# Average pooling over 512 MB: 56 KB blocks in three buffers with a store each, in place of 64 KB loads in two buffers with a store for every four

## The chip, the cores and the metric

The kernel runs on one core of a Trainium2 chip. Three of its engines do work here: VectorE (DVE in the profile), ScalarE (ACT) and SyncE (SP), which only issues transfers. Sixteen DMA engines carry the data between HBM, where input and output lie, and SBUF, the core's own memory of 128 partitions. The metric is the device time of one execution in microseconds (us); lower is better. MB and GB are powers of ten; KB is 1,024 bytes, as in the profile.

## The reference

The input is float32, 64 x 256 x 8192. Each output element is the mean of four neighbours along the last axis, without overlap:

```python
for i in range(out_len):            # out_len = 2048
    start = i * stride              # stride 4, kernel_size 4
    output[:, :, i] = np.mean(x[:, :, start : start + kernel_size], axis=2)
```

So 536.87 MB are read and 134.22 MB are written, and nothing is used twice. Since four neighbours in memory make one output, the input may be cut anywhere at a multiple of four, and the whole problem is one flat array of 134,217,728 elements, 1,048,576 for each partition.

## The kernel before

The flat array is cut into 16 groups. In a group each partition owns 8 rows, that is 256 KB that are contiguous in HBM, and the group is fetched in four loads (`LOADS = 4`, `W = 16384` elements): a load brings 64 KB to each partition, from 128 places that lie 256 KB apart. It makes 8.39 MB. There are 64 such loads; the last of them is split into five pieces (`pieces`: 8192, 4096, 2048, 1024 and 1024 elements for each partition).

For a load, `sums` adds even and odd neighbours on VectorE (line 65, written back over the first half of the input tile), adds even and odd neighbours of that again into the output tile (line 72), and multiplies by 1/4 on ScalarE in place (line 83). The last two pieces are scaled on VectorE instead (line 79). The output tile `ot` holds a whole group, 64 KB for each partition. Only after the group's fourth load, whose second addition is cut into four (`LAST_CUTS`), does one store of 8.39 MB write it out (`store`, line 86). For the last group the store is split into five: one of 4,096 KB while the last loads run, and four more behind them.

All transfers, loads (line 59) and stores (line 86), are issued by SyncE and so go through one DMA queue, in the order in which SyncE gets to them. There are two input tiles (`bufs=2`) and one output tile (`bufs=1`). A load waits until VectorE has read the tile it overwrites: load k+2 is issued when line 72 is done with block k. The first line 72 of a group waits until the store of the group before has landed, because it overwrites the one output tile. Tiles, semaphores and waits come from the framework; the order of issue is the one written in the loop.

Of the kernel before, what the change touches and what calls it, by code (L numbers as in the profile page):

```python
# [1 line left out]

# [4 lines left out]


LOADS = 4

LAST_CUTS = 4


@with_exitstack
def kernel(
    ctx: ExitStack,
    tc: tile.TileContext,
    x: bass.AP,
    kernel_size: bass.AP,
    stride: bass.AP,  # L20
    out: bass.AP,
):
    nc = tc.nc
    K, S = int(kernel_size), int(stride)
    assert K == S == 4
    B, C, L = x.shape
    P = nc.NUM_PARTITIONS
    add = mybir.AluOpType.add
    dt = x.dtype

    per = B * C * L // P
    W = 16384
    G = W * LOADS
    V = W // K
    groups = per // G
    assert per == groups * G

    xf = x.flatten_outer_dims()
    of = out.flatten_outer_dims()
    rows = G // L  # L40
    R = P * rows

    def xg(g):
        return xf[g * R : (g + 1) * R].rearrange("(p f) m -> p (f m)", f=rows)

    def og(g):
        return of[g * R : (g + 1) * R].rearrange("(p f) m -> p (f m)", f=rows)

    pin = ctx.enter_context(tc.tile_pool(name="xin", bufs=2))
    pout = ctx.enter_context(tc.tile_pool(name="res", bufs=1))  # L50

    state = {}

    def load(g, l, a, b):

        if a == 0:
            state["xt"] = pin.tile([P, W], dt, name="xt")
        xt = state["xt"]
        nc.sync.dma_start(out=xt[:, a:b], in_=xg(g)[:, l * W + a : l * W + b])  # L59
        return xt  # L60

    def sums(xt, ot, l, a, b, cuts, scale_on_dve=False):

        h = (a, (a + b) // 2)
        nc.vector.tensor_tensor(  # L65
            out=xt[:, h[0] : h[1]], in0=xt[:, a:b:2], in1=xt[:, a + 1 : b : 2], op=add
        )
        n = (b - a) // K
        for c in range(cuts):
            lo, hi = c * n // cuts, (c + 1) * n // cuts  # L70
            o = ot[:, l * V + a // K + lo : l * V + a // K + hi]
            nc.vector.tensor_tensor(  # L72
                out=o,
                in0=xt[:, a + 2 * lo : a + 2 * hi : 2],
                in1=xt[:, a + 2 * lo + 1 : a + 2 * hi : 2],
                op=add,
            )
            if scale_on_dve:
                nc.vector.tensor_scalar(  # L79
                    out=o, in0=o, scalar1=1.0 / K, scalar2=None, op0=mybir.AluOpType.mult  # L80
                )
            else:
                nc.scalar.mul(o, o, 1.0 / K)  # L83

    def store(g, ot, a, b):
        nc.sync.dma_start(out=og(g)[:, a:b], in_=ot[:, a:b])  # L86

    todo = [(g, l) for g in range(groups) for l in range(LOADS)]  # L90
    last = todo[-1]
    pieces = [W // 2, W // 4, W // 8, W // 16, W // 16]
    tiles = {}
    ot = None
    tiles[0] = load(*todo[0], 0, W)
    tiles[1] = load(*todo[1], 0, W)
    for k, (g, l) in enumerate(todo[:-1]):
        if l == 0:
            held, ot = ot, pout.tile([P, G // K], dt, name="ot")
        sums(tiles.pop(k), ot, l, 0, W, LAST_CUTS if l == LOADS - 1 else 1)  # L100
        if l == LOADS - 1:
            store(g, ot, 0, G // K)
        if k + 2 < len(todo) - 1:
            tiles[k + 2] = load(*todo[k + 2], 0, W)
        elif k + 2 == len(todo) - 1:

            n = pieces[0]
            lt = load(*last, 0, n)
            store(g, ot, 0, (l + 1) * V)
            for w in pieces[1:]:  # L110
                load(*last, n, n + w)
                n += w
    g, l = last
    store(g, ot, (l - 1) * V, l * V)
    edges = [sum(pieces[:i]) for i in range(len(pieces) + 1)]
    for a, b in zip(edges[:3], edges[1:4]):
        sums(lt, ot, l, a, b, 1)
    store(g, ot, l * V, l * V + edges[3] // K)
    for a, b in zip(edges[3:-1], edges[4:]):
        sums(lt, ot, l, a, b, 1, scale_on_dve=True)  # L120
    store(g, ot, l * V + edges[3] // K, (l + 1) * V)


# [1 line left out]
_INS = ['x', 'kernel_size', 'stride']  # L125
_OUTS = [((64, 256, 2048), 'float32')]

_NUMBERS = {'kernel_size': 4, 'stride': 4}


# [26 lines left out]
```

## Time and profile before

| what | value |
|---|---|
| median of 3 runs | 1558.77 us (1558.01 to 1560.35) |
| profiled execution, its time | 1560.02 us |
| profiled execution, its span | 1558.2 us (so 1.8 us lie around it) |
| instructions | VectorE 183, ScalarE 112 |
| DMA packets | 12,532, of which 1,392 under 512 bytes |
| loads / stores issued | 68 / 19, all by SyncE |

The span runs from the first instruction to the last event that the profiler saw. A DMA is split over 16 engines; each engine gets the rows of 8 partitions, one packet for each row, and one packet of 4 bytes that reports completion. So a DMA makes 128 + 16 = 144 packets, and 87 of them make 12,528, which is the packet count of the queue that SyncE uses. In the timeline a row gives the start, the duration, the engine, the line and the tile; in brackets stands the idle time before it and what ended that.

### The profile page before, as it was taken

What the parts mean: (1) busy time and instruction counts of PE and PEld (TensorE: products, weight loads), DVE (VectorE), ACT (ScalarE), POOL (GpSimd) and SP (SyncE); (2) the same over time, 40 slices, a digit from 0 to 9 for tenths busy, and PEclk for the clock granted to TensorE, in tenths of its full rate; (3) what the DMA queues carried; (4) which work ended last, traced back from release to release, by engine and by line L of the source; (5) the groups of instructions that cost most, each with busy time, mean ns of one, the idle gap of its engine ahead of it and who ended that gap; (6) DMA issues with size and microseconds to landing.
All of it is one profiled execution on the core that took longest, in us unless ns stands there. A gap on an engine that the chain in (4) does not pass through costs nothing.

```text
span 1558.2 us, 522 instructions
## 1 busy us (share of the span) xinstructions
DVE 844.0 (54%) x183; ACT 241.9 (16%) x112; POOL 0.2 (0%) x4
## 2 busy tenths in 40 slices
DVE  3654636546365463654636546365463654636546
ACT  1111201112011120111201112011120111201111
POOL 0000000000000000000000000000000000000000
DMA  9999999999999999999999999999999999999998
GB/s 424 437 404 431 442 434 436 434 431 434 429 432 432 439 436 434 432 434 431 431 431 436 436 439 431 434 432 434 431 431 431 431 431 431 431 432 436 426 440 369
DMA packets 12532, 671.13 MB, mean 431 GB/s; under 512 B 1392, under 2 KB 1392, under 8 KB 1776
## 3 DMA queue, kind: packets, MB, share of 16 engines
q1 hardware_dynamic: 12528, 671.09, 99.8%
q14 instruction: 4, 0.03, 0.0%
HBM read 536.87 MB, written 134.22 MB: 431 GB/s over the span
## 4 chain that ended last, share of the span: by engine, by line
DMA 71%; DVE 27%; ACT 1%; SPq 0%; issue 0%
DMA xt<-in_x_dram 71%; DVE xt L65 18%; DVE ot L72 9%; ACT ot L83 1%; SPq L86 0%; SPq L59 0%; DVE ot L79 0%
## 5 line engine op out<-in xcount | busy, mean ns | idle before, releaser
L65 DVE TENSOR_TENSOR xt<-xt 128x8192 f32<-128x8192 f32 (+2 forms) x68 | 556.9, 8190 | 542.5 <-DMA xt<-in_x_dram 542.5
L83 ACT ACTIVATE ot<-ot 128x1024 f32<-128x1024 f32 (+3 forms) x111 | 240.6, 2167 | 1306.1 <-DVE ot L72 1302.6
L72 DVE TENSOR_TENSOR ot<-xt 128x1024 f32<-128x1024 f32 (+4 forms) x113 | 286.9, 2572 | 164.1 <-DMA out_dram<-ot 162.4
L83 ACT ACT_TABLE_LOAD x1 | 1.3, 1283 | 0.7 <-PEq L138 0.7
L79 DVE TENSOR_SCALAR ot<-ot 128x256 f32<-128x256 f32 x2 | 0.6, 291 | 0.0
L138 POOL MEMSET const-bfloat16-1.0<- 128x1 bf16 x1 | 0.1, 101 | 0.0
L138 POOL MEMSET const-uint8-127<- 128x1 uint8 x1 | 0.1, 101 | 0.0
L138 POOL MEMSET const-float32-0.0<- 128x1 f32 x1 | 0.1, 98 | 0.2 <-issue 0.2
L138 POOL MEMSET const-float32-1.0<- 128x1 f32 x1 | 0.1, 98 | 0.0
## 6 DMA issues: line engine op xcount, KB each, us to landing
xt<-in_x_dram SPq DMA_DIRECT2D x1, 4096.0 KB, 17.0
out_dram<-ot SPq DMA_DIRECT2D x1, 4096.0 KB, 23.0
xt<-in_x_dram SPq DMA_DIRECT2D x1, 2048.0 KB, 27.4
out_dram<-ot SPq DMA_DIRECT2D x1, 2048.0 KB, 18.4
out_dram<-ot SPq DMA_DIRECT2D x1, 1792.0 KB, 8.0
xt<-in_x_dram SPq DMA_DIRECT2D x1, 1024.0 KB, 29.4
xt<-in_x_dram SPq DMA_DIRECT2D x2, 512.0 KB, 30.6
xt<-in_x_dram SPq DMA_DIRECT2D x63, 26.9
```

The source lines that it names most:

```text
L65: nc.vector.tensor_tensor(out=xt[:, h[0] : h[1]], in0=xt[:, a:b:2], in1=xt[:, a + 1 : b : 2], op=add)
L72: nc.vector.tensor_tensor(out=o, in0=xt[:, a + 2 * lo : a + 2 * hi : 2], in1=xt[:, a + 2 * lo + 1 : a + 2 * hi : 2], op=add,)
L79: nc.vector.tensor_scalar(out=o, in0=o, scalar1=1.0 / K, scalar2=None, op0=mybir.AluOpType.mult)
L83: nc.scalar.mul(o, o, 1.0 / K)
L138: nc = _bacc.Bacc("TRN2", target_bir_lowering=False, num_devices=1)
```

## The change

The array is now cut into 78 blocks. Each block is contiguous in HBM from its first to its last element: the 128 partitions' rows lie side by side (`"(p m) -> p m"` over a flat slice). A first block of 2,048 elements for each partition is followed by 72 blocks of 14,336 (56 KB for each partition, 7.34 MB) and by a tail of 6144, 4096, 2048, 1280 and 768, which share one input tile and one output tile. There are three input tiles of 56 KB and two output tiles of 14 KB. Every block is stored by itself as soon as ScalarE has scaled it. The stores are issued by ScalarE, behind the multiplication, through ScalarE's own DMA queue; only those of the last full block and of the first tail block are issued by SyncE, behind all loads. Line numbers of the new kernel: load 62, first addition 71, second addition 72, scaling 80 (76 for the last block, on VectorE), store 85.

```diff
-LOADS = 4
-LAST_CUTS = 4
+FULL = 14336
+BUFS_IN = 3
+BUFS_OUT = 2
+HEAD = (2048,)
+TAIL = (6144, 4096, 2048, 1280, 768)
...
-    pin = ctx.enter_context(tc.tile_pool(name="xin", bufs=2))
-    pout = ctx.enter_context(tc.tile_pool(name="res", bufs=1))
+    blocks = [(w, i == 0) for i, w in enumerate(HEAD)]
+    blocks += [(FULL, True)] * (rest // FULL)
+    blocks += [(w, i == 0) for i, w in enumerate(TAIL)]
+    n = len(blocks)
+    first = n - len(TAIL)
+    pin = ctx.enter_context(tc.tile_pool(name="xin", bufs=BUFS_IN))
+    pout = ctx.enter_context(tc.tile_pool(name="res", bufs=BUFS_OUT))
...
+    def load(i):
+        w, fresh = blocks[i]
+        if fresh:
+            load.tile, load.at = pin.tile([P, FULL], dt, name="xt"), 0
+        a = load.at
+        load.at += w
+        src = xf[P * begins[i] : P * begins[i + 1]].rearrange("(p m) -> p m", p=P)
+        xs[i] = load.tile[:, a : a + w]
+        nc.sync.dma_start(out=xs[i], in_=src)
...
+    def store(engine, i, o):
+        dst = of[P * begins[i] // K : P * begins[i + 1] // K]
+        engine.dma_start(out=dst.rearrange("(p m) -> p m", p=P), in_=o)
+
+    loaded = 0
+    for i in range(n):
+        while loaded < n and (loaded < i + BUFS_IN or loaded > first):
+            load(loaded)
+            loaded += 1
+        o = means(i)
+        store(nc.sync if i in (first - 1, first) else nc.scalar, i, o)
```

The arithmetic of a block (`means`) is that of `sums` without cuts: two additions on VectorE and one multiplication, on ScalarE for all blocks but the last.

More of the change, by code (lines that the diff above doesn't have):

```diff
@@ L26 @@
     B, C, L = x.shape
+    assert L % K == 0
     P = nc.NUM_PARTITIONS
+    dt = x.dtype
     add = mybir.AluOpType.add
[L29 to L47, printed above, removed]
@@ L49 @@
-    pin = ctx.enter_context(tc.tile_pool(name="xin", bufs=2))
-    pout = ctx.enter_context(tc.tile_pool(name="res", bufs=1))
[L52 to L64, printed above, removed]
+    xf = x.rearrange("b c l -> (b c l)")
@@ new lines @@
+    of = out.rearrange("b c l -> (b c l)")
+    rest = B * C * L // P - sum(HEAD) - sum(TAIL)
+    assert rest % FULL == 0
+    blocks = [(w, i == 0) for i, w in enumerate(HEAD)]
[5 more added lines that the diff above has]
+    pout = ctx.enter_context(tc.tile_pool(name="res", bufs=BUFS_OUT))
+    xs, begins = {}, [0]
+    for w, _ in blocks:
+        begins.append(begins[-1] + w)
@@ new lines, in load, with means @@
+    def load(i):
[7 more added lines that the diff above has]
+        nc.sync.dma_start(out=xs[i], in_=src)
+    def means(i):
+        w, fresh = blocks[i]
+        if fresh:
+            means.tile, means.at = pout.tile([P, FULL // K], dt, name="ot"), 0
+        a = means.at
+        means.at += w // K
+        o, xt = means.tile[:, a : a + w // K], xs.pop(i)
+        nc.vector.tensor_tensor(out=xt[:, : w // 2], in0=xt[:, ::2], in1=xt[:, 1::2], op=add)
@@ L65, in sums @@
         nc.vector.tensor_tensor(
-            out=xt[:, h[0] : h[1]], in0=xt[:, a:b:2], in1=xt[:, a + 1 : b : 2], op=add
+            out=o, in0=xt[:, : w // 2 : 2], in1=xt[:, 1 : w // 2 : 2], op=add
         )
[L68 to L76, printed above, removed]
-            )
[L78 to L121, printed above, removed]
+        if i == n - 1:
+            nc.vector.tensor_scalar(
+                out=o, in0=o, scalar1=1.0 / K, scalar2=None, op0=mybir.AluOpType.mult
+            )
+        else:
+            nc.scalar.mul(o, o, 1.0 / K)
@@ L125 @@
+        return o
+    def store(engine, i, o):
[8 more added lines that the diff above has]
+        store(nc.sync if i in (first - 1, first) else nc.scalar, i, o)
 _INS = ['x', 'kernel_size', 'stride']
```

## The prediction

> **What bounds the kernel now.** I read the page's busy times and slices first, then its DMA part and its chain of the work that ended last, then that chain in order of time, the groups by shape, and the timeline of the last 30 us.
>
> ```profile
> DVE 844.0 (54%) x183; ACT 241.9 (16%) x112; POOL 0.2 (0%) x4
> ...
> DMA  9999999999999999999999999999999999999998
> GB/s 424 437 404 431 442 434 436 434 431 434 429 432 432 439 436 434 432 434 431 431 431 436 436 439 431 434 432 434 431 431 431 431 431 431 431 432 436 426 440 369
> ...
> q1 hardware_dynamic: 12528, 671.09, 99.8%
> ...
> HBM read 536.87 MB, written 134.22 MB: 431 GB/s over the span
> ```
>
> No compute engine is busy for much more than half of the span, while the 16 DMA engines are busy for 99.8% of it, in every slice. The rate is the same in slices that hold a store and in those that hold only loads. So the DMA engines are the bound, and an edit counts only if it alters the bytes (it doesn't: 671.09 MB before and after), the cost of a packet, or the time in which an engine has no packet.
>
> The chain of work, in order of time, gives the pace:
>
> ```profile
> 567.21 8.70 DVE xt L65
> ...
> 625.20 8.70 DVE xt L65
> ...
> 663.90 8.70 DVE xt L65
> ...
> 760.79 8.70 DVE xt L65
> ...
> 857.49 8.70 DVE xt L65
> ```
>
> Line 65 starts when its load has landed. From 625.20 to 663.90 there are two loads and no store: 19.35 us for 8.39 MB, or 433.5 GB/s. From 567.21 to 663.90, from there to 760.79 and from there to 857.49 each stretch holds four loads and one store, five transfers of 8.39 MB: 96.69, 96.89 and 96.70 us, where five load periods would be 96.75. Over the 13 such stretches from 178.92 to 1439.86 the mean is 97.00, the least is 96.69 (four of them are 96.69 or 96.70) and the greatest is 97.73; the first one, from 80.69, took 98.23. So a store runs at the pace of a load, and turning from loads to a store and back costs nothing by itself in four stretches; the others carry an irregular loss, 0.3 us in the mean. All 14 together lie 5.5 us above 14 times 96.69.
>
> The trace also has a record of each DMA packet. Their median durations are 159 ns for 4,096 bytes, 611 for 16,384, 1,213 for 32,768 and 2,418 for 65,536. From the first to the last 61,440 bytes cost 2,259 ns: 27.2 GB/s for each engine, 435 GB/s for 16. What is left of a packet beyond its bytes is 8.4 ns; the starts of successive packets of one engine lie about 4 ns closer than the durations, so that 4 to 8 ns remain. A completion packet takes 9 ns. At 435.2 GB/s the bytes alone take 1542.0 us: of a span of 1558.2 only 16 us are anything else.
>
> **The change, part by part.**
>
> *Contiguous blocks.* A packet is still one partition's row, now 57,344 bytes in place of 65,536 for a load, 14,336 in place of 65,536 for a store. What may change is the rate at which HBM serves them. The 64 KB packets, taken from places 256 KB apart, run at the same 27.2 GB/s as the 4 KB packets: there is no loss from the layout to win back. I count nothing. The page "DMA: Bandwidth & Descriptors" of the Trainium skill (Latency and other measured facts) says that copies lose rate when the rows of the partitions lie a large power of two apart, 207 in place of 214 GB/s at 512 KiB, and advises to lay tiles out contiguously. By it some of the pitch of 256 KB might be worth up to 3%, an estimate from that page; the 2,418 ns of the packets here show none of it.
>
> *More DMAs.* 68 loads and 19 stores become 78 and 78, so 87 DMAs become 156. Each engine gets 69 x 8 = 552 more data packets and 69 more completion packets: 552 x 4.4 to 8.4 ns = 2.4 to 4.6 us, and 69 x 9 ns = 0.6 us. Together 3.0 to 5.3 us; I take **+4**, for the load period of 19.35 us lies 75 ns above its bytes' 19.275, where eight packets and a completion at 8.4 and 9 ns make 76 and at 4.4 and 9 ns make 44. The same page of the skill (Anatomy of one DMA) has a rule that speaks against the change: a DMA costs about 2.0 us beside its bytes, and DMAs are to be few and large. By it, 69 more DMAs would cost 138 us, an estimate from that page. The rows contradict it for queued DMAs, with 0.08 us each; the 2 us are paid only by a DMA that somebody waits for while nothing else is queued.
>
> *Third input buffer.* VectorE on a block, between the rows of the groups by shape:
>
> ```profile
> L65 DVE TENSOR_TENSOR xt<-xt 128x8192 f32<-128x8192 f32 x63 | 547.6, 8693 | 537.0 <-DMA xt<-in_x_dram 537.0
> L72 DVE TENSOR_TENSOR ot<-xt 128x4096 f32<-128x4096 f32 x48 | 212.4, 4425 | 163.5 <-DMA out_dram<-ot 162.4
> L83 ACT ACTIVATE ot<-ot 128x4096 f32<-128x4096 f32 x48 | 173.6, 3616 | 1103.5 <-DVE ot L72 1103.5
> ```
>
> With 4,418 ns for 4,096 elements at line 65, and 2,292 and 1,909 for 2,048 at lines 72 and 83, the sizes 7,168 and 3,584 come to 7.62 + 3.89 = 11.5 us on VectorE and 3.2 on ScalarE. A block's transfers take (7.34 + 1.84 MB) / 433.5 = 21.2 us. Load i+2 goes out when VectorE is done with block i-1, 11.5 us after that landed; load i then has 9.7 us to run and load i+1 is queued whole. So the queue never empties by some 30 us. Before, the margin was 19.35 - 13.1 = 6.2 us (line 65 waits about 6.2 us for each load); it too was enough, so the third buffer removes no idle time: 0 us. Were this cover gone, each microsecond of lateness beyond 30 would cost one per block, 72 in all.
>
> *Stores on ScalarE's queue.* The waits of SyncE's store for ScalarE (339.1 us in 18 times) leave SyncE's order. They held back loads, as at 95.17, where the store goes out before the next load; but DMA stayed busy through it, so 0 us come back. On ScalarE a store's issue waits for its own multiplication, and behind it stands only the next multiplication, some 20 us later. Line 72 waited 162.4 us for the landing of the one output tile; this goes, and it was hidden. Two output tiles are enough: a store goes out about 15 us after its block landed, and its tile is wanted 2 x 21.2 + 7.6 = 50 us after. Even if its packets alternate one for one with load packets, it runs for the whole 21 us of a period; 14 us remain.
>
> What the trace does not show is two queues that feed an engine at once. From below: a second queue could hide what lies between packets, at most the 16 us by which the span exceeds its bytes, less about 3 for start and end: -13. From above: the irregular losses could come with each store, 5.5 / 14 = 0.39 us, and 63 more stores would cost 25. A price for every packet that alternates is excluded by the four stretches without loss. I take 0, the nearest row: both directions were in flight in the last 25 us before too, at the same packet durations.
>
> *The tail.* Before:
>
> ```profile
> 1549.63 0.29 DVE L79 TENSOR_SCALAR ot<-ot 128x256 f32<-128x256 f32 x1
> 1549.83 0.42 DVE L72 TENSOR_TENSOR ot<-xt 128x256 f32<-128x256 f32 x1
> 1550.29 0.29 DVE L79 TENSOR_SCALAR ot<-ot 128x256 f32<-128x256 f32 x1
> ```
>
> VectorE ends 7.7 us before the span does; in that time the engines write the last two stores, and by the packet records the last engine ends some 2 us after most. After: let A be the landing of the last full block. The tail's loads land by A + 21, with the store before them in between. VectorE does the last full block until A + 11.5 and the tail's pieces until about A + 25. The stores that SyncE and ScalarE issue from A + 15 on keep the engines busy until A + 29.6 (8.4 us for 3.67 MB behind the loads). VectorE is done 5 us before that, so the tail stays full. I count 0, and the same unevenness of the engines as before.
>
> **Sum.** Span 1558.2 + 4 = 1562.2 us, the profiled execution's time 1560.0 + 4 = 1564.0. The median of the runs lies 1.25 below that execution, so I predict **1562.8 us**, 0.26% slower. About 0.2%, 3.1 us, is what a measurement of this kernel can tell from no change: 1555.7 to 1561.9 count as the same.
>
> **Rivals.**
>
> 1. *The irregular losses shrink* (not slower). They stand at the stores; many small contiguous stores, spread evenly, may avoid them. For it: 98.23 and 97.73 beside 96.69 at the same work. Against: nothing says what they are. If all 5.5 us go, the time is 1558.8 + 4 - 5.5 = 1557.3, the same. It decides as soon as more than 0.9 us of them go.
> 2. *Faster.* Beyond these losses, the last engines' 2 us go as well and the packets cost only 3.0: 1558.8 + 3.0 - 7.5 = 1554.3. With the gaps between packets hidden by the second queue it could reach 1546.
> 3. *Every store brings its loss*: 0.39 us x 63 = 25, so 1587; half of that is 1575. For it: the losses stand where a store starts or ends. Against: four stretches without any.
> 4. *The queue runs dry*, because stores take more than twice a period and VectorE waits for output tiles. Against: 14 us of margin there and 30 at the loads. 1 us for each of 72 blocks would be 1635.
> 5. *The change does nothing* but rearrange a saturated resource, packet costs overlapping too: 1558.8, the same.
>
> **Chances.** The forecast, 1560 to 1566: 0.43, of which 0.31 slower and 0.12 the same. Rivals 1 and 5 together, 1555.7 to 1560: 0.25, the same. Rival 2: 0.13, faster. Rival 3: 0.15, and rival 4: 0.04, slower. So faster 0.13, the same 0.37, slower 0.50. The range leaves out most of rival 2, the upper half of rival 3 and rival 4: 1555 to 1575.
>
> **What would show it.** In the profile after: 22,464 packets in the two queues (156 x 144), DMA at 9 in every slice, 431 GB/s or a little under; line 71 waiting for its load and for nothing else, one block each 21.2 us; no wait of line 72 for a store; packets of 57,344 bytes at about 2.12 us and of 14,336 at 0.535. Wrong are: packets longer than that (rival 3), gaps in DMA (rival 4), a block period under 21.1 us (rival 2).

## The result, and the profile after

| | median | range | runs |
|---|---|---|---|
| before | 1559.51 us | 1558.01 to 1560.35 | 20 |
| after | 1556.57 us | 1556.35 to 1556.79 | 20 |

After takes 0.9982 of the time of before (95% interval 0.9977 to 0.9988): 2.9 us or 0.18% less, where 0.26% more was forecast. The time lies inside the predicted range and inside what the prediction called the same. It also scatters less, by 0.4 us in place of 2.3. The page of the profile after answers to the first lines shown of before:

```profile
DVE 843.6 (54%) x157; ACT 235.1 (15%) x78; POOL 0.2 (0%) x4
...
DMA  9999999999999999999999999999999999999999
GB/s 411 437 426 429 443 432 425 442 440 418 441 440 419 440 441 421 436 443 425 431 443 427 429 442 435 422 442 441 417 440 441 422 435 443 423 433 439 432 428 395
...
q1 hardware_dynamic: 11520, 539.50, 80.2%
q10 hardware_dynamic: 10944, 131.60, 19.8%
...
HBM read 536.87 MB, written 134.22 MB: 432 GB/s over the span
```

The DMA engines are the bound as before. There are now two queues, SyncE's (q1) and ScalarE's (q10), with 22,464 packets between them. The last slice, 369 GB/s before, has 395. The view of waits lists what stopped VectorE:

```profile
DVE xt L71 <- DMA xt<-in_x_dram: 697.3, 73, 15.4
...
DVE ot L72 <- DVE xt L71: 0.4, 1, 0.4
```

The second addition waits for no store any more; the first one waits for its load, and that is all. In VectorE's timeline the loads land in an even beat:

```profile
612.58 7.62 DVE L71 TENSOR_TENSOR xt<-xt 128x7168 f32<-128x7168 f32 x1 [9.57 <-DMA xt<-in_x_dram]
...
633.74 7.62 DVE L71 TENSOR_TENSOR xt<-xt 128x7168 f32<-128x7168 f32 x1 [9.55 <-DMA xt<-in_x_dram]
...
654.91 7.62 DVE L71 TENSOR_TENSOR xt<-xt 128x7168 f32<-128x7168 f32 x1 [9.56 <-DMA xt<-in_x_dram]
```

A period is 21.17 us for 9.18 MB, whose bytes alone take 21.08 at 435.2 GB/s: 0.09 us for a block's two DMAs, sixteen data packets and two completions on each engine. Load packets still take 2.116 us and store packets 0.535, and by their records an engine takes one of each in turn.

Since the engines hardly ever rest, the right account is the time that bytes do not explain: at each moment, the time since the start of the span less the bytes moved so far at 435.2 GB/s. From the packet records of one profiled execution each (us); a packet counts as too long when it takes 0.1 us or more beyond its bytes at 27.2 GB/s and 8.4 ns:

```
                    at 240  at 480  at 1200  at 1545  last packet | packets 0.1 us or more too long
before                4.8     5.7     9.0      12.3      15.0     |   169
after                 4.1     5.2     8.2       9.9      11.4     |    33
e1_stores_on_sync     5.4     6.9    10.0      11.7      15.0     |   124
e3_two_inputs         4.3     5.3     8.3      10.0      11.5     |    47
e4_half_loads         4.8     6.5    11.6      14.1      16.9     |    50
e8_pairs              4.3     5.0    14.9      22.5      26.5     |   509
e9_64k_blocks         4.5     5.4     8.1       9.6      11.1     |    72
e10_pairs_56k         5.5     8.0    13.7      16.2      18.2     |   460
e12_half_blocks       5.0     7.0    13.1      15.9      18.4     |    51
e13_body_on_sync      5.3     6.6     9.9      11.6      13.9     |   138
e14_tail_on_sync      4.2     5.3     8.3      10.0      12.5     |    43
```

After is ahead of before by 0.7 us at 240, by 0.8 at 1200, by 2.5 at 1545 and by 3.6 at the end. In the long middle, 240 to 1200, both lose the same 4.1 us. The difference is made before 240, after 1200, and in the last 10 us.

The same records split it into three parts. What the packets too long take beyond their due, summed and divided by 16 engines, is 5.2 us in before and 0.7 in after: 4.5 less. What is left of the account at 1545 is 7.1 and 9.1: 2.0 more, for 69 more DMAs. In the last 10 us an engine stands idle for 2.4 us in the mean in before and for 1.1 in after: 1.3 less.

### The profile page after: what moved, and what is told of

Read it like the earlier page. It is cut to its first block, busy times and chain, and to the rows that moved or that the text cites. A ratio compares the mean times of both kernels' runs of the same rounds, so it can differ in the third digit from the quotient of the medians.

```text
span 1554.7 us, 658 instructions
## 1 busy us (share of the span) xinstructions
DVE 843.6 (54%) x157; ACT 235.1 (15%) x78; POOL 0.2 (0%) x4
## 4 chain that ended last, share of the span: by engine, by line
DVE 53%; another core or an unknown queue 42%; DMA 5%; issue 0%; DVEq 0%; SPq 0%
DVE xt L71 35%; DVE ot L72 18%; DMA xt<-in_x_dram 5%; DVEq L72 0%; SPq L62 0%; DVE ot L76 0%
## 5 line engine op out<-in xcount | busy, mean ns | idle before, releaser
L71 DVE TENSOR_TENSOR xt<-xt 128x7168 f32<-128x7168 f32 (+3 forms) x78 | 558.4, 7160 | 697.3 <-DMA xt<-in_x_dram 697.3
L80 ACT ACTIVATE ot<-ot 128x3584 f32<-128x3584 f32 (+3 forms) x77 | 233.8, 3037 | 1311.7 <-DVE ot L72 1311.7
L72 DVE TENSOR_TENSOR ot<-xt 128x3584 f32<-128x3584 f32 (+3 forms) x78 | 285.4, 3660 | 7.0 <-DVE xt L71 0.4
```

Source lines behind the costliest of these rows:

```text
L71: nc.vector.tensor_tensor(out=xt[:, : w // 2], in0=xt[:, ::2], in1=xt[:, 1::2], op=add)
L72: nc.vector.tensor_tensor(out=o, in0=xt[:, : w // 2 : 2], in1=xt[:, 1 : w // 2 : 2], op=add)
```

## The experiments

Three theories at first. **Q**: ScalarE's own queue removes the irregular losses, since the engines no longer turn from loads to stores as a body. **L**: the contiguous layout does. **B**: the third input buffer does. Each experiment ran beside the kernel before on one chip; ratios are to that. After itself ran only for the result, so "more than after" compares medians from different sessions; the medians of before in them lie between 1558.2 and 1559.7.

**e1_stores_on_sync.** All stores back in the loads' queue:

```diff
-        store(nc.sync if i in (first - 1, first) else nc.scalar, i, o)
+        store(nc.sync, i, o)
```

> The kernel after, with every store issued by SyncE, so that loads and stores share one queue again. Theory Q (two queues: packets of loads and stores alternate, so the engines never turn from one direction to the other as a body, and the irregular losses of before vanish): the losses come back, 1560 to 1564 us and slow packets at each store. Theory L (the contiguous layout removed them) and theory B (the third input buffer, a load always queued well ahead): as after, 1556 to 1557.5.

1560.24 us, ratio 1.0008 (0.9999 to 1.0017): 3.7 us slower than after, as Q said. But the run was not as clean as its expectation supposed. Its timeline ends so:

```profile
1542.74 1.50 DVE L71 TENSOR_TENSOR xt<-xt 128x640 f32<-128x640 f32 x2 [0.32 <-DMA xt<-in_x_dram]
1548.10 4.17 DVE L72 TENSOR_TENSOR ot<-xt 128x1536 f32<-128x1536 f32 x5 [3.85 <-DMA out_dram<-ot]
1549.89 3.31 ACT L80 ACTIVATE ot<-ot 128x1536 f32<-128x1536 f32 x4 [12.76 <-DVE ot L72]
1551.40 4.22 SPq L85 DMA_DIRECT2D out_dram<-ot  x5
1552.30 0.26 DVE L76 TENSOR_SCALAR ot<-ot 128x192 f32<-128x192 f32 x1
```

The tail's loads are issued together, and in the one queue a store stands behind them; the tail's output tile is free only when that store has landed, at 1548. VectorE is done at 1552.6, in place of 1548.0 in after. So e1 holds two effects; e13 and e14 part them below.

**e2_strided_rows.** The full blocks taken from groups in which each partition owns 224 KB:

```diff
+        group = flat[at : at + P * Q // k].rearrange("(p m) -> p m", p=P)
+        return group[:, l * FULL // k : (l + 1) * FULL // k]
```

> The kernel after, with the full blocks taken four at a time from a group in which each partition owns 224 KB, so that a load's rows lie 224 KB apart and a store's 56 KB apart; sizes, queues and buffers as after. Theory L: the losses come back in full, 1560 to 1564 us. Theories Q and B: as after, 1556 to 1557.5.

1556.46 us, ratio 0.9981 (0.9972 to 0.9990), as after. L falls: rows 224 KB apart cost nothing here. The 256 KB of before were not run in the new kernel; for them there are only before's packets, 2,418 ns for 64 KB.

**e3_two_inputs.** `BUFS_IN = 2`.

> The kernel after with two input buffers in place of three. A load then goes out 11.5 us after its forerunner landed, with 9.7 us of the next load still to run. Theory B: losses come back, above 1559 us. Theories Q and L: as after, 1556 to 1557.5, since the queue of loads never empties.

1556.55 us, ratio 0.9983 (0.9974 to 0.9991), as after. B falls.

**e4_half_loads.** Each full load cut into two DMAs:

```diff
-        nc.sync.dma_start(out=xs[i], in_=src)
+            nc.sync.dma_start(out=xs[i][:, : w // 2], in_=src[:, : w // 2])
+            nc.sync.dma_start(out=xs[i][:, w // 2 :], in_=src[:, w // 2 :])
```

> The kernel after with each full load cut into two DMAs of 28 KB for each partition: 72 more DMAs, 576 more data packets for each engine. This measures the price of a DMA, which the prediction took as 44 to 76 ns. By 44 ns 3.2 us more than after, about 1559.8; by 76 ns 5.5 us more, about 1562; if a second queue hides the gaps between packets, under 1 us more.

1562.10 us, 5.5 more than after: 77 ns for each added load, of which the account shows some 60 in the body and the rest at the end.

Then Q was tried in the frame of the kernel before, against a rival **S**: the small, frequent store is what helps, in whatever queue.

**e5_each_sync and e6_each_scalar.** Before, with a store after each load, from SyncE or from ScalarE:

```diff
-        if l == LOADS - 1:
-            store(g, ot, 0, G // K)
+        if g < groups - 1:
+            store(g, ot, l * V, (l + 1) * V)                # e5
+            nc.scalar.dma_start(out=og(g)[:, l * V : (l + 1) * V], in_=ot[:, l * V : (l + 1) * V])  # e6, in its place
```

> The kernel before, with a store of 16 KB for each partition after each load (in all groups but the last), issued by SyncE as before: 45 more DMAs, 3.5 us at 77 ns each. Theory Q (two queues): the losses stay, 1559.6 + 3.5 = 1563 us. Rival S (the small, frequent store removes the losses, the queue does not matter): 1559.6 + 3.5 - 6 = 1557.

> The same as e5_each_sync, but these stores are issued by ScalarE on its own queue. Theory Q: the losses go, 1559.6 + 3.5 - 6 to 8 = 1555 to 1557 us, at least 4 us less than e5_each_sync. Rival S: the same time as e5_each_sync.

e5 took 1562.12 us, ratio 1.0042 (1.0018 to 1.0066), with runs from 1558.7 to 1576.0: no gain in time from small stores by themselves, and S falls. e6 took 1698.38, ratio 1.0896 (1.0882 to 1.0911). Neither theory had that. The DMA part of e5's page has for these stores (count, KB each, median us to landing):

```profile
out_dram<-ot SPq DMA_DIRECT2D x61, 2048.0 KB, 12.2
```

The same part of e6's page:

```profile
out_dram<-ot ACTq DMA_DIRECT2D x60, 2048.0 KB, 35.1
```

And the view of waits of e6:

```profile
DVE ot L72 <- DMA out_dram<-ot: 251.8, 15, 16.9
```

Here a store that shares the engines with loads, one packet each, lands nearly three times as late. The kernel before has one output tile for four blocks: line 72 then waits for the last store of the group, the next load goes out late because line 72 frees its tile, and with two input tiles the engines run empty (396 GB/s over the span). This is the prediction's rival 4, in another kernel.

**e7_big_scalar.** Before, the 15 big stores from ScalarE's queue:

```diff
-            store(g, ot, 0, G // K)
+            nc.scalar.dma_start(out=og(g), in_=ot)
```

> The kernel before with nothing changed but the queue of the 15 stores of 8.39 MB: ScalarE issues them. No DMA is added. Theory Q alone: the losses go at no price, 1552 to 1554 us. Against it stands the one output tile: the store now shares the engines with loads one packet each and takes about 39 us in place of 19, so line 72 waits for it and the next load may go out too late; if that shows, 1555 us or more, with a long wait of line 72 and gaps in the DMA slices.

1672.15 us, ratio 1.0717 (1.0702 to 1.0733). The wait of line 72 that was feared came, 403.5 us in 15 times or 26.9 each, where before has 10.8. It says nothing of Q.

**e8_pairs.** A version meant to be better: 64 KB blocks, two blocks to a store.

```diff
-FULL = 14336
-BUFS_IN = 3
+FULL = 16384
+BUFS_IN = 2
...
+            if full(i) % 2:
+                nc.scalar.dma_start(out=dst, in_=means.tile)      # 32 KB for each partition
```

> A new version: blocks of 64 KB for each partition in two input buffers, the stores of two blocks joined (32 KB for each partition) in two output buffers, ScalarE's queue, head and tail as after: 107 DMAs in place of 156. By 77 ns for each of the 49 DMAs less than after it takes 3.8 us less, 1552.8; by 44 ns 2.2 less, 1554.4. If small stores are what removes the losses, 1556 or more.

1569.64 us, ratio 1.0071 (1.0059 to 1.0083), with no wait for any store. So **Q as I had put it fell**: a second queue with ample buffers, and the account shows 22.5 us unexplained at 1545, 509 packets too long. They stand where a store sets in, that is, where its first packets go out: from 647 to 655, say, where the engines take up the store issued at 643.8. A store of 32 KB packets runs for 29 of the 49 us of a pair and then stops. In after a store takes 8 x 2.645 = 21.2 us, as long as its block: the stream of stores never stops. That was theory **C**, the losses come where a stream of stores sets in or stops, with rival **P**: packets of 64 KB beside a second queue are to blame.

Not every set-in costs, though. Of e8's 31, the first one made 16 load packets too long, 1.0 us of each engine's time. The next ten, from 115 to 550 us, have two such packets between them, and at 480 the account of e8 stands at 5.0, not above after's 5.2. The loss starts at about 600 and is then some 0.7 us for each store.

**e9_64k_blocks.** After with `FULL = 16384`, `BUFS_IN = 2`, a store for each block.

> The kernel after with blocks of 64 KB for each partition in two input buffers, and still one store for each block (16 KB for each partition) from ScalarE's queue: 138 DMAs in place of 156. Theory C (the losses stand where a stream of stores sets in or stops; a store for each block, in a queue of its own, lasts as long as the block's load, so that it never stops): no losses, 18 DMAs less at 77 ns, 1555.2 us. Rival P (the losses of e8_pairs came from packets of 64 KB beside a second queue): 1560 us or more.

1555.89 us, ratio 0.9983 (0.9974 to 0.9992). No losses with 64 KB packets: P falls. The 18 DMAs saved don't show in the ratio, so it is no better version that can be told from after.

**e10_pairs_56k.** e3 with the stores of two blocks joined as in e8.

> e3_two_inputs (56 KB blocks, two input buffers) with the stores of two blocks joined, 28 KB for each partition; 36 DMAs less. The store now runs for some 25 us of the 42 us of a pair. Theory C: the losses come with each of the 36 stores, 0.3 to 0.5 us each as in e8_pairs, so 1556.6 - 2.8 + 11 to 18 = 1565 to 1572. Rival P: none, 1553.8.

1563.82 us, ratio 1.0032 (1.0021 to 1.0044): 7.3 more than e3, with 36 DMAs less. Theory C had the direction, its size was a little high. The beat shows the store's set-in and stop, 42.5 us for the pair shown:

```profile
612.17 7.62 DVE L82 TENSOR_TENSOR xt<-xt 128x7168 f32<-128x7168 f32 x1 [5.37 <-DMA xt<-in_x_dram]
...
637.72 7.62 DVE L82 TENSOR_TENSOR xt<-xt 128x7168 f32<-128x7168 f32 x1 [13.94 <-DMA xt<-in_x_dram]
...
654.67 7.63 DVE L82 TENSOR_TENSOR xt<-xt 128x7168 f32<-128x7168 f32 x1 [5.40 <-DMA xt<-in_x_dram]
```

One load shares the engines with the store and takes 25.5 us, the next has them to itself and takes 16.95.

Of the time lost in packets too long, 84% in e8 and 82% in e10 lie within 6 us of a store's first packet, about an eighth of the time. So it is the set-in of a joined store that costs, not its whole run, and at the stop the records show no loss. But theory C is too wide, and e4 shows it. There a load's packets are half as large, so that a store's eight packets are through after 8 x (1.062 + 0.535) = 12.8 us of a block's 21.2. The DMA part of e4's page has for these stores:

```profile
out_dram<-ot ACTq DMA_DIRECT2D x71, 1792.0 KB, 16.8
```

The page of after:

```profile
out_dram<-ot ACTq DMA_DIRECT2D x71, 1792.0 KB, 27.6
```

The stream of e4 stops and sets in again with each of these stores, and after 100 us e4 has six packets too long in all. A stop by itself costs nothing there. The joined stores also have packets twice as large, longer pauses, and loads whose rows lie 128 KB (e8) or 112 KB (e10) apart; which of these makes a set-in cost, no run separates.

**e11_loads_alone.** No stores of the body:

```diff
-        store(nc.sync if i in (first - 1, first) else nc.scalar, i, o)
+        if not 1 <= i < first - 1:
+            store(nc.sync if i in (first - 1, first) else nc.scalar, i, o)
```

> The kernel after without the stores of the head and the full blocks except the first block and the last full one: 71 outputs of 1.84 MB are computed and not written, 85 DMAs and 540.8 MB remain, in one queue almost throughout. By 435.2 GB/s the bytes take 1242.6 us; with 85 DMAs at 77 ns, start, end and what lies around the span (5.5 us) 1254.6 us. If one queue loses time even without any turn from loads to stores, 1258 us or more; theory C: 1254 to 1255.

1256.82 us, all runs within 0.02: 2 us over the estimate and over theory C's 1254 to 1255, but under the rival's bound. Its timeline:

```profile
616.90 7.62 DVE L71 TENSOR_TENSOR xt<-xt 128x7168 f32<-128x7168 f32 x1 [5.32 <-DMA xt<-in_x_dram]
...
633.86 7.63 DVE L71 TENSOR_TENSOR xt<-xt 128x7168 f32<-128x7168 f32 x1 [5.34 <-DMA xt<-in_x_dram]
...
650.79 7.62 DVE L71 TENSOR_TENSOR xt<-xt 128x7168 f32<-128x7168 f32 x1 [5.31 <-DMA xt<-in_x_dram]
```

Loads alone in one queue keep a period of 16.945 us, 79 ns over their bytes' 16.866, and after the first 53 us only four packets are too long.

**e12_half_blocks.** `FULL = 7168`, four input and four output buffers: twice the loads and twice the stores.

> The kernel after with blocks of 28 KB for each partition in four input and four output buffers (the tail's five pieces in two tiles): 72 more loads, 72 more stores of 7 KB packets, and the stream of stores still runs as long as the loads. This prices a store DMA where e4_half_loads priced a load. If a load costs 77 ns beyond its bytes and a store beside it almost nothing (10 ns, from the block periods of after and of e11_loads_alone), 6.3 us more than after, 1562.8. If both cost 77, as the prediction had it, 11.1 more, 1567.7. If the second queue hides half of both, 6.2, which this run can't tell from the first.

1563.85 us, ratio 1.0037 (1.0023 to 1.0050): 7.3 more than after by the medians, 8.6 by the ratios, for 72 loads and 72 stores; e4 has 5.5 by either for 72 loads alone. So a store added to a running stream costs some 25 to 43 ns ((7.3 or 8.6 less 5.5) / 72), a load 77. Both at 77, 11.1 us, is too much. The ratios' intervals are 1 to 2 us wide to each side, so the price of a store is no sharper than that. The account at 1545, without the packets too long, has 57 ns for a load (e4) and 21 for a store (e12).

**e13_body_on_sync and e14_tail_on_sync** part the two effects of e1:

```diff
-        store(nc.sync if i in (first - 1, first) else nc.scalar, i, o)
+        store(nc.sync if i < first - 2 or i in (first - 1, first) else nc.scalar, i, o)   # e13
+        store(nc.sync if i >= first - 2 else nc.scalar, i, o)                             # e14
```

> e1_stores_on_sync mixed two things: the stores of the body in the loads' queue, and, at the end, a store behind the tail's loads, for which line 72 waits until 1548 us. Here only the body's stores (up to the fourth block from its end and the third) are issued by SyncE; the last three full blocks' and the tail's are issued as in after. If the body's own queue is what counts, all of e1's 3.7 us remain, 1560.2. If the body costs what its packet records show up to 1545 us, 1.8, then 1558.4. If it costs nothing, 1556.6.

> The counterpart: the body's stores from ScalarE's queue as in after, those of the last two full blocks and of the tail from SyncE behind all loads, as in e1_stores_on_sync. If e1's tail costs what its records show after 1545 us, 1.8, then 1558.4; if all of e1's loss is the body's, 1556.6; if all of it is the tail's, 1560.2. The two runs' excesses over after should add up to e1's 3.7.

e13: 1559.25 us, ratio 0.9999 (0.9991 to 1.0008), 2.7 more than after. e14: 1557.57, ratio 0.9985 (0.9976 to 0.9994), 1.0 more. Together 3.7, as e1. By the ratios it is 2.7 and 0.5, and the interval of e14 reaches after's; its trace shows a loss all the same. In e14's view of waits stands the tail's wait for its output tile:

```profile
DVE ot L72 <- DMA out_dram<-ot: 2.1, 1, 2.1
```

Just behind it, from 1547.5 to 1550, its engines are busy for 0.23 of the time, those of after for 0.98.

In e13 the packets too long sum to 2.5 us for an engine, 1.8 more than in after, and the rest of the account at 1545 is 9.1 in both. So up to there all that the body's own queue saves is packets too long; a store's DMA costs the same in either queue. The other part shows at the end: in the last 10 us an engine of e13 stands idle for 1.8 us in the mean, one of after for 1.1. That fits how far apart the 16 engines end one and the same load, by the records of the completion packets. In after that is 0.4 us at the start, 0.9 at 1000 and 1.75 at 1520. In e13 it grows from 0.3 to 3.0 within 270 us and stays at 3.3; in before it grows from 0.8 to between 2.6 and 3.8. The execution ends with its last engine.

## Why the prediction was wrong

*What bounds the kernel*: right. DMA is at 9 in all 40 slices, and of the experiments that kept DMA busy and wrote the whole output the largest move is 0.7% (e8).

*Contiguous blocks, 0*: right, as far as e2 shows. The measured 64 KB packets had said so. The Trainium skill's page "DMA: Bandwidth & Descriptors" (Latency and other measured facts), from which a gain of up to 3% had been estimated, has 512 KiB as the smallest pitch in its row on the pitch; rows 224 KB apart cost nothing here.

*More DMAs, +4 us*: **failed in size.** The 44 to 76 ns were read from a load's period and packets and given to 59 stores and 10 loads alike. For loads they hold (16.945 us against 16.866 in e11; 77 ns in e4). A store in a running stream costs some 25 to 43 ns (e12): 10 x 77 + 59 x 25 to 43 ns = 2.2 to 3.3 us; the account has 2.0 up to 1545. Why a load costs two to three times as much is not shown. That a second queue's packets fill the pause between two loads is not it: with the body's stores in the loads' queue the account without the packets too long is the same, 9.1 (e13). The 2.0 us for a DMA of the same page of the skill (Anatomy of one DMA) are given there for DMAs that GpSimd issues, while SyncE and ScalarE issue those here; a queued one costs 0.02 to 0.08 us by e4 and e12.

*Third input buffer, 0*: right (e3). The block's times came out as worked out, 7.62, 3.89 and 3.19 us.

*Stores on ScalarE's queue, 0, and two queues at once, 0*: **this step failed**, and with it the forecast of slower. Whether the irregular losses would stay was the open question, and I left them as they were. The reason given, "the nearest row", was one queue in every row. That holds too for the four stretches without loss, which were to exclude a price for packets that alternate: none alternate there. (There is no such price: 2.645 us for the two in after.) e13 and e14 measure the second queue at 2.7 us in the body and 1.0 in the tail. Rival 1 described most of what came: it put the time at 1557.3 if all irregular losses went, and 1556.6 was measured, with 4.5 of before's 5.2 us of packets too long gone. That the numbers lie so close is in part luck: in the last 10 us, which it left out, an engine idles 1.3 us less, and the DMAs cost 2 to 3 us in place of 4. Its reason, many small and contiguous stores spread evenly, was only in part right: contiguity has no share (e2), and small stores in the loads' queue gain no time (e5). A second queue alone is not enough either: with the stores joined in pairs it is slower than one queue, by 5.5 us (e10) and 10.4 (e8) against before, where a store for each block gains (e3, e9). That the stream then runs without a stop is not what decides (e4).

*The tail, 0*: its timing was right. VectorE ended 24.2 us after the last full block landed (25 predicted), the last packet came 29.6 after (29.6 predicted). But "the same unevenness of the engines" was wrong: after 1545 before loses 2.7 us, after 1.5. Part of it is not unevenness: before's tail was not full, for from 1547.5 to 1550 its engines are busy for 0.78 of the time, after's for 0.98. (Before writes its last group in four stores, of 4,096, 2,048, 1,792 and 256 KB, not in five.) And the tail's cover was not priced: with its stores in the loads' queue the margin of 5 us is gone and 1.0 us lost (e14), because the output tile is then waited for. The prediction priced such a loss of cover for the loads alone.

So the sum: 2.2 to 3.3 us more for DMAs, and 3.7 less through the second queue, make -0.4 to -1.5. The measured -2.9 leaves 1.4 to 2.5 us to what else differs. e1, all of the change but the queue, stands by its ratio 1.2 us over before, with an interval of -0.2 to +2.7, so this rest is hardly resolved by times. The packet records place it: of the 4.5 us of packets too long that went, 1.8 came with the body's queue (e13); the other 2.7 are gone in e13 too, which has the body's stores in the loads' queue. The late losses of before (0.9 us from 1200 to 1500 and 0.8 from 1500 to 1545 more than after) are the larger part. The turns around before's big stores are where they stand, but no run changed those alone without running the engines empty.

What stays open is the cause inside the engines: why packets grow longer when a stream of stores sets in, and why not at every set-in. In the body on one queue it happens at the first turns, where all 16 engines are hit at once (15 or 16 packets of 0.1 to 0.7 us too much at 36.6 and 54.4 in e13 and e1), and fades by about 440 us, when they stand more than 3 us apart. That the distance protects them is not shown: in e8 ten set-ins cost nothing with the engines mostly within 1 us of each other at the end of a load, and later ones cost 0.7 us with the engines 1.5 us apart and more.

## What to carry to other kernels

When DMA is busy throughout, count three things: bytes, a price for each DMA taken from the same direction, and the turns between loads and stores. Try the stores in a queue of their own, with a store for each block. Stores joined in pairs cost 0.2 to 0.3 us each here (e10) to 0.5 (e8) in the mean, far more than the DMAs that they save, and the reason is open. Before moving stores to a second queue, recompute when their tile comes free: they land at the pace of the shared engines, here 35 us in place of 12, and a single output tile then cost 9%.

## What the runs showed that I had not expected

- Two queues share an engine packet by packet, not byte by byte: 57,344 bytes, then 14,336, 2.645 us for the two. The smaller packets' queue so gets a fifth of the bytes, here just what it needed. The Trainium skill's page "DMA: Bandwidth & Descriptors" (Queues, rings and completion order) says that an engine goes round its queues by packets, and the records agree; here a packet was a partition's whole row of up to 65,536 bytes.
- The 16 DMA engines keep no step. In e13 they drift from 0.3 to 3.0 us apart in 270 us and are still 3.3 apart at 1500, so none waits for the others within the queue, and the end belongs to the last.
- The time of after repeats to 0.4 us over 20 runs; before scatters by 2.3, e5 by 17 over 12.
